# A gate table built from bfloat16 one-hots, with the gate split into three bfloat16 parts

## The chip, the cores and the metric

The kernel runs on one core of one Trainium2 chip. The metric is the device time of one execution in microseconds (us). A core has four compute engines with queues of their own, which run in order and wait for each other through semaphores: TensorE (PE in the profile, with its weight loads as PEld), VectorE (DVE), ScalarE (ACT) and GpSimd (POOL). SyncE (SP) issues most of the DMAs. [...]

## The reference, cut to what matters

One layer over 1024 frames of width 1024: two token mixers side by side (RWKV-7 and S5), then a mixture of 16384 single-neuron experts of which each of 8 heads picks 16 per frame, then a norm. The change lies in the expert part, between the choice of experts and their use.

```python
def _rms_norm(x, gain): ...                      # x * rsqrt(mean(x*x) + 1e-6) * gain
...
h = x                                             # (1, 1024, 1024)
p = _rms_norm(h, norm_mix) @ w_in                 # RWKV columns | S5 columns | two gates
y_a = _rwkv7_time_mix(p_rwkv, ...)                # recurrence over frames, 8 heads x 64
y_b = _s5_ssm_glu(p_s5, ...)
h = h + (g_a * y_a + g_b * y_b) @ w_out
h = h + _peer_ffn(_rms_norm(h, norm_ffn), ...)
return _rms_norm(h, norm_final)

def _peer_ffn(xn, wq, subkeys, table_u, table_v): # per block of 128 frames xt
    q = (xt @ wq).reshape(PEER_BLOCK, PEER_HEADS, 2, PEER_HALF)
    s = jnp.einsum('thcd,hcnd->thcn', q, subkeys)
    sv, si = lax.top_k(s, PEER_TOPK)              # 16 of 128 keys, on both sides
    cand = sv[:, :, 0, :, None] + sv[:, :, 1, None, :]
    cv, ci = lax.top_k(cand.reshape(PEER_BLOCK, PEER_HEADS, 256), PEER_TOPK)
    i1 = jnp.take_along_axis(si[:, :, 0], ci // PEER_TOPK, axis=-1)
    i2 = jnp.take_along_axis(si[:, :, 1], ci % PEER_TOPK, axis=-1)
    e = i1 * PEER_KEYS + i2                       # one of 128*128 experts
    gate = jax.nn.softmax(cv, axis=-1)
    hid = jax.nn.gelu(jnp.einsum('td,thkd->thk', xt, table_u[e]))
    return jnp.einsum('thk,thkd->td', gate * hid, table_v[e])
```

## The kernel before

The frames lie in eight blocks of 128. For the blocks 1 to 5 (`DB`) the experts are computed densely: every one of the 16384 experts is applied to all 640 frames, and a table of gates, zero where an expert was not chosen, weighs the result. The blocks 0, 6 and 7 (`GB`) fetch the rows of the chosen experts by indirect DMA instead, row by row.

`gate_table` makes the table of one dense block. For frame t the 128 chosen pairs (first key, second key) lie on the 128 partitions; a matrix product of two one-hot matrices, one of them scaled by the gates, adds each gate into its place of a 128 x 128 grid of experts. Four frames (`TG`) go at a time; such a step is called a group below, and there are 32 groups in a block and 160 in all. In a group VectorE compares an iota with the second keys (`oaq`) and with the first keys (`ohq`), in bfloat16; ScalarE copies `oaq` into the float32 tile `oha` in another order of axes; GpSimd or VectorE multiplies `ohq` by the gates `gT` into the float32 tile `ohb`; TensorE multiplies, one float32 product per frame, into the PSUM tile `gm`; ScalarE copies `gm` into a part of `stg`. Every eight groups `stg` (2 MB) is stored to the DRAM tensor `gd`.

No order is written out by hand. The functions run as streams of a planner, the class `Weave`, which has a cost for each instruction, keeps a queue time for each engine, and emits whichever ready instruction could start first, by a bonus for its stream where several could. `nc.copy` leaves the choice of ScalarE or VectorE to it, `nc.either` that of VectorE or GpSimd. The streams that matter here are `table` (the gate tables, bonus 2.0), `top` (the choice of experts, bonus 1.2), `front`, `pre` and `state` (the RWKV recurrence, 16 items, bonus 1.5 to 3.0) and `dense`.

`dense_stream` waits in the planner for the end of the RWKV streams. It then loads the frames `dx` (10 loads of 0.5 MB) and, chunk by chunk, the experts' first vectors `ur`; it splits each into `uh` (ScalarE) and `ul` (the rest, `ur - uh`), and computes the scores `S` of a chunk of 128 experts in 48 products. Scores of the first four chunks may run before the tables are done; `weigh` then multiplies the scores by the gates `G`, read back from `gd`, and the products into `acc` follow:

```python
            for _ in range(GV):
                next(X["ds"])

            wv.wait(lambda: {"tables", "top"} <= flags)
```

There are 128 chunks. The last instructions of an RWKV item are a group norm: the tile `ob`, its mean and variance (`m`, `rtrg`), the normed tile `yc`, eight small products `rs<-cst,yc`, and `y`, which SyncE stores to `ygd`.

Of the kernel before, what the change touches and what calls it, by code (L numbers as in the profile page):

```python
# [19 lines left out]
F32 = mybir.dt.float32  # L20
F32R = mybir.dt.float32r
BF = mybir.dt.bfloat16
# [3 lines left out]
OP = mybir.AluOpType  # L26
# [17 lines left out]
TG = 4  # L44
# [329 lines left out]
class Kern:  # L374
# [1147 lines left out]
    def gate_table(self, blk, e, g, pool):  # L1522


        nc, v = self.nc, self.nc.vector
        p = self.ps("gp", [128, 3, 128], 1, self.psg)
        for i, src in enumerate((e[:, :, 0], e[:, :, 1], g)):
            x = pool.tile([128, 128], F32, name=self.nm("slc"), tag="slc", bufs=1)
            nc.copy(x.rearrange("p (h k) -> p h k", h=8), src)
            nc.tensor.transpose(p[:, i], x, self.ident)  # L1530
        iT = pool.tile([128, 2, 128], BF, name=self.nm("iT"), tag="iT", bufs=2)
        gT = pool.tile([128, 128], F32, name=self.nm("gT"), tag="gT", bufs=2)
        nc.copy(iT, p[:, 0:2])
        nc.copy(gT, p[:, 2])
        for t32 in range(4):
            stg = pool.tile([128, 128, 32], F32, name=self.nm("stg"), tag="stg", bufs=2)
            for t16 in range(32 // TG):
                t0 = 32 * t32 + TG * t16
                shp = [128, 128, TG]
                bc = lambda x: x[:, None, t0:t0 + TG].to_broadcast(shp)  # L1540
                a, b = (pool.tile([128, TG, 128], F32, name=self.nm("oh" + x), tag="oh" + x, bufs=3) for x in "ab")
                turn = lambda x: x.rearrange("p t m -> p m t")
                bq = pool.tile(shp, BF, name=self.nm("ohq"), tag="ohq", bufs=2)
                aq = pool.tile(shp, BF, name=self.nm("oaq"), tag="oaq", bufs=2)
                v.tensor_tensor(aq, self.iotaM, bc(iT[:, 1]), op=OP.is_equal)
                nc.copy(turn(a), aq)
                v.tensor_tensor(bq, self.iotaM, bc(iT[:, 0]), op=OP.is_equal)
                nc.either("tensor_tensor", turn(b), bq, bc(gT), op=OP.mult)
                for t4 in range(TG // 4):
                    ps = self.ps("gm", [128, 4, 128], GMB, self.psg)  # L1550
                    for i in range(4):
                        t = 4 * t4 + i
                        nc.tensor.matmul(ps[:, i], a[:, t], b[:, t], start=True, stop=True)
                    o = TG * t16 + 4 * t4
                    nc.copy(stg[:, :, o:o + 4].rearrange("p i t -> p t i"), ps)
            nc.sync.dma_start(self.gd[4 * DB.index(blk) + t32], stg)
        self.tabled += 1

# [545 lines left out]
```

## Time and profile before

| | |
|---|---|
| median of 3 runs | 3673.98 us (3672.0 to 3679.5) |
| the profiled execution's own time | 3668.73 us |
| its span, first to last instruction | 3666.8 us |
| time outside the span | 1.9 us |
| granted clock of TensorE, mean | 0.944 |
| busy share PE / DVE / ACT / POOL | 90% / 77% / 38% / 33% |

The shares are means over stages with different limits. The gate tables are made between 1268 and 1635 us of the span, beside the end of the RWKV recurrence and of the choice of experts; the dense experts fill the time from there to the end. [...]

### The profile page before, as it was taken

The page shows a single profiled execution, that of the slowest core. Times are in us where ns is not written, and L with a number is a line of the kernel's source. Part 1 is how long each engine was busy: PE and PEld are TensorE (multiplying, and loading weights), DVE is VectorE, ACT ScalarE, POOL GpSimd, SP SyncE. Part 2 cuts the span into 40 slices and gives each one's busy share as a digit, 9 for nine tenths or more (in the row PEclk, how much of TensorE's full clock was granted, in tenths as well). Part 3 has the DMA queues.
Part 4 walks back from the last instruction along what each step waited for, and adds up shares of the span by engine and source line. Part 5 has one row for each costly group of instructions (what it writes and reads, how often), then busy time and mean ns, then how long its engine had stood idle before and what let it go on. Part 6 is the DMA issues. An engine that isn't in the chain of part 4 may idle for free.

```text
span 3666.8 us, 59750 instructions
## 1 busy us (share of the span) xinstructions
PE 3317.5 (90%) x22415; PEld 2841.2 (77%) x22415; DVE 2807.3 (77%) x6159; ACT 1398.3 (38%) x2906; POOL 1205.8 (33%) x1127
## 2 busy tenths in 40 slices
PE   7999999998888877778998889989999999999996
PEld 7777787767667766667887778878899998998985
DVE  7546412536989999956888968898888888888887
ACT  4322323323332398872333323323333333333333
POOL 3553323533443255432223222222222222223221
PEclk9899999998989898899999899989999999999998
DMA  5541223455567532268997789777898888988985
GB/s 207 199 165 64 87 91 114 136 174 176 194 238 258 181 126 116 117 203 296 330 329 275 266 311 346 281 278 284 296 326 304 320 317 317 323 305 293 323 298 219
DMA packets 359952, 869.10 MB, mean 237 GB/s; under 512 B 28960, under 2 KB 175520, under 8 KB 307952
## 3 DMA queue, kind: packets, MB, share of 16 engines
q1 hardware_dynamic: 303792, 461.01, 37.1%
q0 software_dynamic: 55296, 402.68, 29.3%
q8 instruction: 176, 2.88, 0.3%
q10 hardware_dynamic: 576, 1.61, 0.1%
q14 instruction: 112, 0.92, 0.1%
HBM read 759.16 MB, written 104.86 MB: 236 GB/s over the span
## 4 chain that ended last, share of the span: by engine, by line
PE 37%; DVE 25%; issue 16%; DMA 9%; ACT 6%; POOL 6%; SPq 1%; POOLq 0%; DVEq 0%; ACTq 0%
PE S L170 10%; PE acc L170 10%; PE mm L170 7%; POOL row L170 5%; PE tps L170 3%; DMA G<-gd 2%; DVE gacc L170 2%; DMA vr<-in_uv_dram 2%; ACT stg L170 2%; ACT oha L170 2%; PE rs L170 2%; PE gl L170 2%; DVE row L170 1%; PE pp L170 1%; PE rw L170 1%
## 5 line engine op out<-in xcount | busy, mean ns | idle before, releaser
L170 POOL DMA_INDIRECT row<-in_uv_dram,ei x384 | 524.8, 1367 | 1481.4 <-DVE gacc L170 1240.8
L170 PE MATMUL S<-dx,uh 128*128 128x320 f32 x4096 | 783.7, 313 | 14.1 <-ACT uh L170 7.5
L170 PEld LDWEIGHTS S<-dx,uh 128*128 128x128 f32 x4096 | 653.6, 190 | 32.6 <-ACT uh L170 9.9
L170 PE MATMUL acc<-vh,wh 128*128 128x512 f32 x1280 | 505.9, 403 | 55.8 <-DVE acc L170 49.0
L170 DVE SCALAR_TENSOR_TENSOR gacc<-row,hid,gacc 128x1024 f32<-128x1024 f32 x384 | 491.5, 1280 | 63.8 <-ACT hid L170 63.3
L170 PE MATMUL acc<-vl,wh 128*128 128x512 f32 x1280 | 513.2, 401 | 9.5 <-DVE vl L170 9.5
L170 PE MATMUL acc<-vh,wl 128*128 128x512 f32 x1280 | 509.7, 398 | 0.0
L170 PE MATMUL S<-dx,ul 128*128 128x320 f32 x2048 | 476.0, 313 | 19.3 <-DVE ul L170 15.4
L170 DVE CUSTOM_DVE_ANT_0 row<-row,gx 128x1024 f32<-128x1024 f32 x384 | 469.4, 1223 | 16.0 <-DMA row<-in_uv_dram,ei 15.8
L170 PEld LDWEIGHTS S<-dx,ul 128*128 128x128 f32 x2048 | 345.8, 190 | 25.6 <-DVE ul L170 19.1
L170 PEld LDWEIGHTS acc<-vh,wh 128*128 128x128 f32 x1280 | 245.1, 192 | 120.0 <-DVE acc L170 54.2
L170 ACT ACTIVATE hid<-hid 128x1 f32<-128x1 f32 x384 | 77.1, 201 | 576.6 <-DVE hid L170 576.0
L170 PEld LDWEIGHTS acc<-vl,wh 128*128 128x128 f32 x1280 | 246.7, 193 | 59.9 <-DVE vl L170 13.0
L170 PEld LDWEIGHTS acc<-vh,wl 128*128 128x128 f32 x1280 | 246.5, 193 | 54.9 <-issue 2.2
L170 ACT ACTIVATE vh<-vr 128x512 fp32r<-128x512 f32 x256 | 160.4, 627 | 315.4 <-PE acc L170 171.1
L170 PE MATMUL gm<-ohb,oha 128*128 128x128 f32 x1280 | 200.4, 308 | 57.3 <-ACT stg L170 38.2
L170 DVE TENSOR_TENSOR vl<-vr,vh 128x512 fp32r<-128x512 f32 x256 | 177.2, 693 | 90.3 <-ACT vh L170 88.3
L170 PEld LDWEIGHTS gm<-ohb,oha 128*128 128x128 f32 x1280 | 174.8, 213 | 75.7 <-issue 35.1
L170 DVE TENSOR_TENSOR acc<-acc,acc 128x512 f32<-128x512 f32 x320 | 213.6, 683 | 12.3 <-PE acc L170 11.7
L170 POOL TENSOR_TENSOR ohb<-ohq,gT 128x512 f32<-128x512 bf16 x126 | 151.5, 1204 | 155.0 <-DVE ohq L170 101.7
L170 PE MATMUL mm<-xnH,wh 128*128 128x512 f32 x480 | 196.3, 409 | 6.2 <-DVE pm L170 6.2
L170 PE MATMUL mm<-xnH,wl 128*128 128x512 f32 x480 | 194.7, 406 | 0.7 <-POOL wl L170 0.7
(443 smaller groups left out, 6280.9 us busy)
## 6 DMA issues: line engine op xcount, KB each, us to landing
ur<-in_ut_dram SPq DMA_DIRECT2D x128, 512.0 KB
vr<-in_uv_dram SPq DMA_DIRECT2D x256, 256.0 KB
wf<-wsd SPq DMA_DIRECT2D x120, 512.0 KB
gd<-stg SPq DMA_DIRECT2D x20, 2048.0 KB
G<-gd SPq DMA_DIRECT2D x31, 1280.0 KB
wsd<-sw SPq DMA_DIRECT2D x40, 512.0 KB
wr<-in_wc_dram SPq DMA_DIRECT2D x30, 512.0 KB
wr<-in_wg_dram SPq DMA_DIRECT2D x32, 256.0 KB
```

The lines of the kernel that those rows point to most:

```text
L170: op.alts = [(e, self.cost(e, n, outs, ins), lambda f=f, a=a, k=k: f(*a, **k)) for e, n, f, a, k in alts]
```

## The change

The two keys are compared in one VectorE instruction of 1024 elements, whose result `ohq` holds both one-hots in bfloat16. The gate is split, once per block, into three bfloat16 parts that add up to it (`gT`, with the rests `gr`); one VectorE instruction of 1536 elements multiplies the first one-hot by all three (`ohb`, also bfloat16). TensorE takes both as they lie, without the copies in another order of axes, and adds the three products of a frame in PSUM. The copy of `gm` into `stg` now reads PSUM in steps of 128 elements and writes runs of four, where before it read in order and wrote single elements 32 apart. The buffers of `ohq` and `ohb` are four each.

```diff
--- before.py
+++ after.py
@@ -1529,30 +1529,32 @@
             nc.copy(x.rearrange("p (h k) -> p h k", h=8), src)
             nc.tensor.transpose(p[:, i], x, self.ident)
         iT = pool.tile([128, 2, 128], BF, name=self.nm("iT"), tag="iT", bufs=2)
-        gT = pool.tile([128, 128], F32, name=self.nm("gT"), tag="gT", bufs=2)
+        gT = pool.tile([128, 3, 128], BF, name=self.nm("gT"), tag="gT", bufs=2)
         nc.copy(iT, p[:, 0:2])
-        nc.copy(gT, p[:, 2])
+        r = p[:, 2]
+        for k in range(3):
+            nc.copy(gT[:, k], r)
+            if k < 2:
+                r2 = pool.tile([128, 128], F32, name=self.nm("gr"), tag=f"gr{k}", bufs=1)
+                v.tensor_tensor(r2, r, gT[:, k], op=OP.subtract)
+                r = r2
         for t32 in range(4):
             stg = pool.tile([128, 128, 32], F32, name=self.nm("stg"), tag="stg", bufs=2)
             for t16 in range(32 // TG):
                 t0 = 32 * t32 + TG * t16
-                shp = [128, 128, TG]
-                bc = lambda x: x[:, None, t0:t0 + TG].to_broadcast(shp)
-                a, b = (pool.tile([128, TG, 128], F32, name=self.nm("oh" + x), tag="oh" + x, bufs=3) for x in "ab")
-                turn = lambda x: x.rearrange("p t m -> p m t")
-                bq = pool.tile(shp, BF, name=self.nm("ohq"), tag="ohq", bufs=2)
-                aq = pool.tile(shp, BF, name=self.nm("oaq"), tag="oaq", bufs=2)
-                v.tensor_tensor(aq, self.iotaM, bc(iT[:, 1]), op=OP.is_equal)
-                nc.copy(turn(a), aq)
-                v.tensor_tensor(bq, self.iotaM, bc(iT[:, 0]), op=OP.is_equal)
-                nc.either("tensor_tensor", turn(b), bq, bc(gT), op=OP.mult)
+                bc = lambda x: x[:, :, None, t0:t0 + TG].to_broadcast([128, x.shape[1], 128, TG])
+                oh = pool.tile([128, 2, 128, TG], BF, name=self.nm("ohq"), tag="ohq", bufs=4)
+                gb = pool.tile([128, 3, 128, TG], BF, name=self.nm("ohb"), tag="ohb", bufs=4)
+                v.tensor_tensor(oh, self.iotaM[:, None].to_broadcast([128, 2, 128, TG]), bc(iT), op=OP.is_equal)
+                v.tensor_tensor(gb, oh[:, 0:1].to_broadcast([128, 3, 128, TG]), bc(gT), op=OP.mult)
                 for t4 in range(TG // 4):
                     ps = self.ps("gm", [128, 4, 128], GMB, self.psg)
                     for i in range(4):
                         t = 4 * t4 + i
-                        nc.tensor.matmul(ps[:, i], a[:, t], b[:, t], start=True, stop=True)
+                        for k in range(3):
+                            nc.tensor.matmul(ps[:, i], oh[:, 1, :, t], gb[:, k, :, t], start=k == 0, stop=k == 2)
                     o = TG * t16 + 4 * t4
-                    nc.copy(stg[:, :, o:o + 4].rearrange("p i t -> p t i"), ps)
+                    nc.copy(stg[:, :, o:o + 4], ps.rearrange("p t i -> p i t"))
             nc.sync.dma_start(self.gd[4 * DB.index(blk) + t32], stg)
         self.tabled += 1
 
```

The planner makes a new order from this. The rows below are those of the program's order, before and after.

**VectorE, where the first table begins** (`ti`, `tv`, `t` belong to the choice of experts, `cs`, `cc`, `k`, `f`, `X`, `ob`, `yc` to RWKV). Before:

```order
L170 TENSOR_TENSOR oaq_13718<-iotaM,iT_13712 128x512
L170 TENSOR_TENSOR ohq_13717<-iotaM,iT_13712 128x512
L170 TENSOR_TENSOR oaq_13723<-iotaM,iT_13712 128x512
L170 TENSOR_TENSOR ohq_13722<-iotaM,iT_13712 128x512
L170 SCALAR_TENSOR_TENSOR cs_13766<-sreset,sa_13023 128x256
L170 TENSOR_TENSOR oaq_13798<-iotaM,iT_13712 128x512
L170 TENSOR_TENSOR cc_13767<-cs_13766 128x4x64
L170 TENSOR_TENSOR ohq_13795<-iotaM,iT_13712 128x512
L170 TENSOR_SCALAR cc_13767<-cs_13766 128x4
L170 SCALAR_TENSOR_TENSOR k_13771<-sa_13023,cols 128x256
```

And now:

```order
L170 TENSOR_TENSOR gr_13714<-gp_13674,gT_13713 128x128
L170 TENSOR_TENSOR ohq_13717<-iotaM,iT_13712 128x1024
L170 TENSOR_TENSOR ohq_13720<-iotaM,iT_13712 128x1024
L170 TENSOR_TENSOR gr_13715<-gr_13714,gT_13713 128x128
L170 TENSOR_TENSOR ohq_13723<-iotaM,iT_13712 128x1024
L170 SCALAR_TENSOR_TENSOR cs_13764<-sreset,sa_13023 128x256
L170 TENSOR_TENSOR ohb_13718<-ohq_13717,gT_13713 128x1536
L170 TENSOR_TENSOR ohb_13721<-ohq_13720,gT_13713 128x1536
L170 TENSOR_TENSOR ohb_13724<-ohq_13723,gT_13713 128x1536
L170 TENSOR_TENSOR ohq_13842<-iotaM,iT_13712 128x1024
L170 TENSOR_TENSOR cc_13765<-cs_13764 128x4x64
L170 TENSOR_TENSOR ohb_13843<-ohq_13842,gT_13713 128x1536
```

Before, two gate rows alternate with one to three rows of other streams all through the stage. Now 57 gate rows follow this piece with one row between them, and so it goes on: the tables of blocks 1 to 3 stand nearly without other work on VectorE, then some 230 rows of RWKV and of the choice of experts without a gate row, then the tables of blocks 4 and 5.

**VectorE, the end of the last RWKV item.** Before, the normed tile `yc` stands 81 gate rows ahead of the last one:

```order
L170 TENSOR_TENSOR rtrg_16491<-rtrg_16491 128x4 x2
L170 SCALAR_TENSOR_TENSOR rtrg_16491<-rtrg_16491 128x4
L170 TENSOR_TENSOR oaq_16819<-iotaM,iT_16276 128x512
L170 TENSOR_TENSOR ohq_16818<-iotaM,iT_16276 128x512
L170 TENSOR_TENSOR yc_16490<-ob_16246,rtrg_16491 128x256
L170 COPY slc_16833<-e_15958 128x128
L170 TENSOR_TENSOR oaq_16861<-iotaM,iT_16855 128x512
```

Now it stands behind the last gate row of all, `ohb_17917`:

```order
L170 TENSOR_REDUCE m_17448<-ob_17248 128x4
L170 TENSOR_TENSOR ohb_17917<-ohq_17916,gT_17307 128x1536
L170 TENSOR_SCALAR m_17448<-m_17448 128x4
L170 TENSOR_TENSOR ob_17248<-ob_17248,m_17448 128x256
L170 TENSOR_REDUCE m_17448<-yc_17449 128x4
L170 TENSOR_SCALAR m_17448<-m_17448 128x4
...
L170 TENSOR_TENSOR yc_17449<-ob_17248,rtrg_17450 128x256
L170 TENSOR_TENSOR vl_18146<-vr_18121,vh_18145 128x512
```

The dots stand for the eleven short operations that compute `rtrg`. On TensorE the eight products `rs<-cst,yc` of this item, and behind them the first score product, stand directly behind the last `gm` product; before, 29 rows of `S` stood among the `gm` rows.

**SyncE, the store of the last RWKV tile and the loads for the dense experts.** Before, the loads stand ahead of the last four stores of the table:

```order
L170 DMA gd<-stg_16696 128x4096
L170 DMA ygd_81<-y_16708 128x2x128
L170 DMA dx_16905<-xtT_84 128x8x128
...
L170 DMA ur_16907<-in_ut_dram 128x1024
L170 DMA gd<-stg_16857 128x4096
L170 DMA gd<-stg_16998 128x4096
L170 DMA ur_17158<-in_ut_dram 128x1024
L170 DMA gd<-stg_17111 128x4096
L170 DMA gd<-stg_17252 128x4096
```

Now they stand behind the last one:

```order
L170 DMA gd<-stg_17643 128x4096
L170 DMA gd<-stg_17789 128x4096
L170 DMA ygd_81<-y_17554 128x2x128
L170 DMA dx_18005<-xtT_84 128x8x128
...
L170 DMA ur_18007<-in_ut_dram 128x1024
L170 DMA ur_18023<-in_ut_dram 128x1024
L170 DMA ur_18058<-in_ut_dram 128x1024
L170 DMA vr_18121<-in_uv_dram 128x512
```

All ten `dx` loads and the four `ur` loads moved behind the twentieth store of the table and behind `ygd<-y`. From the first score on, GpSimd's order is the same as before, and that of the other engines nearly so.

## Rows read from the trace of the kernel before

**Rows 1.** Stretches: us; busy us (count) of PE PEld DVE ACT POOL; clock, DMA, GB/s.

```profile
1200.00:1267.00 67.00, 54.95 (x491) 48.52 (x489) 64.56 (x322) 17.52 (x41) 17.45 (x16) 0.82 0.66 220
1267.00:1560.00 293.00, 223.99 (x2143) 190.82 (x2143) 280.89 (x705) 263.32 (x353) 162.43 (x132) 0.90 0.28 112
1560.00:1635.00 75.00, 51.67 (x330) 45.27 (x329) 46.40 (x82) 64.60 (x76) 25.29 (x20) 0.89 0.62 205
2500.00:3500.00 1000.00, 987.71 (x5530) 897.30 (x5530) 865.26 (x1159) 351.14 (x828) 273.51 (x202) 1.00 0.87 312
```

**Rows 2.** Costliest groups, 1267 to 1640 us: what, count, busy us, mean ns, idle.

```profile
L170 PE MATMUL gm<-ohb,oha 128*128 128x128 f32 x1280 | 200.4, 308 | 57.3 <-ACT stg L170 38.2 <-DVE ohb L170 10.0 <-POOL ohb L170 6.5
L170 ACT ACTIVATE stg<-gm 128x512 f32<-128x512 f32 x160 | 180.4, 1142 | 16.1 <-PE gm L170 16.0
L170 ACT ACTIVATE oha<-oaq 128x512 f32<-128x512 bf16 x158 | 178.7, 1153 | 9.9 <-DVE oaq L170 9.6
L170 POOL TENSOR_TENSOR ohb<-ohq,gT 128x512 f32<-128x512 bf16 x126 | 151.5, 1204 | 155.0 <-DVE ohq L170 101.7 <-ACT sa L170 12.5 <-PE gm L170 8.0
L170 DVE TENSOR_TENSOR oaq<-iotaM,iT 128x512 bf16<-128x512 bf16 x160 | 100.9, 631 | 23.0 <-ACT oha L170 18.6 <-ACT iT L170 4.1
L170 DVE TENSOR_TENSOR ohq<-iotaM,iT 128x512 bf16<-128x512 bf16 x160 | 83.3, 521 | 1.0 <-POOL ohb L170 1.0
```

**Rows 3.** Timeline of ScalarE, 1589 to 1591 us: start, duration, what.

```profile
1589.10 1.17 ACT L170 ACTIVATE stg<-gm 128x512 f32<-128x512 f32 x1
1590.00 1.18 ACT L170 ACTIVATE oha<-oaq 128x512 f32<-128x512 bf16 x1
```

**Rows 4.** Timeline of VectorE at four places, with idle time in brackets.

```profile
1216.01 0.69 DVE L170 TENSOR_TENSOR oh<-rb,io 128x1024 bf16<-128x1024 bf16 x1
1216.61 0.15 DVE L170 TENSOR_SCALAR mst<-mst 128x1 f32<-128x1 f32 x1
...
1430.35 0.41 DVE L170 TENSOR_TENSOR oaq<-iotaM,iT 128x512 bf16<-128x512 bf16 x1
1430.69 0.41 DVE L170 TENSOR_TENSOR ohq<-iotaM,iT 128x512 bf16<-128x512 bf16 x1
...
1563.55 0.43 DVE L170 TENSOR_TENSOR oaq<-iotaM,iT 128x512 bf16<-128x512 bf16 x1 [3.64 <-ACT iT L170]
```

**Rows 5.** Timeline of TensorE: a `gm` group, the first and last scores, the first `acc`.

```profile
1440.93 1.16 PE L170 MATMUL gm<-ohb,oha 128*128 128x128 f32 x8
...
1601.12 0.85 PE L170 MATMUL S<-dx,uh 128*128 128x320 f32 x4 [0.61 <-ACT uh L170]
...
1653.26 0.57 PE L170 MATMUL S<-dx,uh 128*128 128x320 f32 x2 [0.38 <-ACT w L170]
...
1660.42 0.39 PE L170 MATMUL acc<-vh,wh 128*128 128x512 f32 x1
```

**Rows 6.** Timeline of the end of the last RWKV item, all engines.

```profile
1563.57 0.81 ACT L170 ACTIVATE y<-rs,cols 128x128 f32<-128x128 f32 x2
1564.45 0.78 POOL L170 TENSOR_TENSOR y<-y,bo 128x256 f32<-128x256 f32 x1 [4.62 <-ACT y L170]
1567.49 0.40 DVE L170 TENSOR_TENSOR y<-y,g 128x256 f32<-128x256 f32 x1
1567.97 0.37 SPq L170 DMA_DIRECT2D ygd<-y  x1
```

**Rows 7.** Timeline of SyncE's queue, and the last split of `ur`.

```profile
1568.45 16.29 SPq L170 DMA_DIRECT2D dx<-xtT  x10
1584.79 1.77 SPq L170 DMA_DIRECT2D ur<-in_ut_dram  x1
...
1646.14 0.33 SPq L170 DMA_DIRECT2D ur<-in_ut_dram  x1
...
1649.99 1.06 ACT L170 ACTIVATE uh<-ur 128x1024 fp32r<-128x1024 f32 x1 [5.79 <-DMA ur<-in_ut_dram]
...
1651.12 2.39 POOL L170 TENSOR_TENSOR ul<-ur,uh 128x1024 fp32r<-128x1024 f32 x1 [5.01 <-DMA G<-gd]
```

## The prediction

> **What bounds the kernel now.** I read the stretches first, because the shares over the whole span mix stages. From 2500 to 3500 us TensorE is busy 987.71 of 1000 us at the full clock [rows 1]: the dense experts are TensorE's, and whatever moves their start moves the end. The tables are made before that. From 1267 to 1560 us VectorE is busy 280.89 of 293 us and ScalarE 263.32; from 1560 to 1635 us VectorE falls to 46.40 of 75 and ScalarE stays at 64.60 [rows 1]. So the stage has two limits, VectorE while the choice of experts and RWKV still run beside the table, and ScalarE behind that.
>
> The groups of the stage say what fills them: on ScalarE the copies `oha` (178.7 us) and `stg` (180.4 us), on VectorE `oaq` and `ohq` with 160 instructions each, on GpSimd 126 `ohb` [rows 2]. The timeline gives the pace: a `stg` starts 0.90 us ahead of the `oha` behind it [rows 3], so a group of four frames costs ScalarE 1.80 us where it is the limit. On VectorE an `oaq` of 512 elements starts 0.34 us ahead of the next instruction when nothing disturbs it [rows 4], but the means are 631 and 521 ns [rows 2]: that is the stretch under GpSimd's work.
>
> What follows the stage matters as much. Scores need `dx` and `ur`, and before the change these are issued from 1568.45 us on, right behind `ygd<-y` at 1567.97 [rows 6, 7], 65 us ahead of the end of the stage. The first score runs at 1601.12 us, beside the tables, and the first `acc` at 1660.42 [rows 5]. That moment is what I forecast.
>
> **The change on VectorE.** 512 elements take 0.34 us and 1024 elements, of the same type and kind, 0.60 [rows 4], so another 512 cost 0.26 and 1536 cost 0.86. A group takes 0.60 + 0.86 = 1.46 us and 160 groups 234 us. The ten `gr` of 128 elements at some 0.3 add 3 us. The other work on VectorE: 705 + 82 instructions in the stage [rows 1], less 356 for the gates (160, 160, 34 `ohb`, 2 copies), leave 431; by the new order some 20 of them go to GpSimd, so 410. A like mix without gates cost 64.56 us for 322 instructions between 1200 and 1267 us [rows 1], 0.20 each: 82 us. About 3 us of it lie behind the last gate row. Without waits VectorE's last gate row would end at 1267 + 4 (the wait for the first `iT`, 4.1 us [rows 2]) + 234 + 3 + 79 = 1587 us.
>
> Waits come on top. In the new order the tables of blocks 1 to 3 lie together, then some 230 rows without a gate row, then blocks 4 and 5. At each of the last two blocks VectorE waits for the chain to `iT`, 3.64 us the last time [rows 4]: 7 us. In the middle piece (46 us of work) nothing fills the gaps of the recurrence and of the one-hot sums that GpSimd multiplies. The bounds are 2 us, by the 96% that VectorE was busy from 1200 to 1267 us, and 25, if it idled a third of the time; I take 12, nearer the first, since that stretch had this kind of work too. The last gate row then ends at 1587 + 7 + 12 = 1606 us.
>
> **The change on the other engines, at nothing.** ScalarE loses `oha` and keeps `stg`. Reading PSUM in steps is not in the trace. Below, 512 elements cost half of the 1.06 us of a plain copy of 1024 [rows 7]; above, I allow twice the present 0.90 us [rows 3]. I take 0.9, as the writes get easier and the reads harder: it hides behind VectorE's 1.46. At 1.8 it would not, and cost (1.8 - 1.46) x 160 = 54 us.
>
> [...]
>
> TensorE does 12 products of 128 columns per group instead of 8 (a float32 product is two in the trace: 1280 for 640 frames [rows 2]). Now 8 cost 1.16 us [rows 5], 0.145 each. [...] The bounds are 0.72 (128/320 of a score product) and 12 x 0.145 = 1.74 us. I take 0.83, as a bfloat16 product needs one pass like the score: hidden. [...] At 1.74 it costs 0.28 x 160 = 45 us. GpSimd's 151.5 us [rows 2] vanish; it was no limit, and what it gives back is counted in the undisturbed prices. The two extra copies and the rests `gr` per block lie ahead of the need, but for the waits above.
>
> **The work that the new order moves out.** The last RWKV item's `yc` stands behind the last gate row. Behind it come three long operations and some thirteen short ones, at 0.4 and 0.15 us [rows 4, 6], with one trip to ScalarE: about 5 us. Then `rs`, `y` on ScalarE (0.81), on GpSimd (0.78) and on VectorE (0.40) [rows 6], with the hops 3.5 us. So `ygd<-y` is issued 8 us behind the last gate row, and everything behind it in SyncE's queue waits: ten `dx` in 16.29 us, then `ur` [rows 7]. From the issue of a `ur` to its copy `uh` 3.85 us pass (1646.14 to 1649.99 [rows 7]). With a store of 2 MB just ahead, the first score starts about 8 + 17 + 4 + 2 = 31 us behind the last gate row. There is one buffer for `ur`: a load (3.85), `uh` (1.06) and `ul` (2.39) [rows 7] make 7.3 us a chunk, as much as its 48 products (7.16 [rows 5]). Four chunks and the wait for the first `ul` make 33 us. The first `acc` comes 64 us behind the last gate row. Nothing else can fill this on TensorE.
>
> **The sum.** First `acc` at 1606 + 64 = 1670 us, against 1660.4: 10 us later. The dense order is nearly the same from there on and TensorE-bound, so all of it reaches the end: 3668.7 of the profiled execution become 3679. That execution lies 5.3 us below the median of the runs, so I forecast 3674 + 10 = 3684 us. A measurement can tell about 0.2%, 7.3 us, from no change.
>
> **Rivals.**
> *The lost overlap is paid back, no change.* If the waits come to 10 instead of 19 us, or the tail to 55, the two nearly cancel: 3670 to 3681. VectorE's 96% speaks for it; that the middle piece has no filler speaks against it.
> *VectorE's other work gets cheap, faster.* Those 410 instructions may cost 0.15 instead of 0.20 us with less of GpSimd beside them, as `oaq` at 0.34 against a mean of 631 ns suggests [rows 2, 4]. That is 20 us less: the last gate row at 1586, the end at 3664. It decides from 17 us on. Against it: from 1200 to 1267 us, whence the 0.20, GpSimd was busy 17.45 of 67 us only [rows 1].
> *A new limit in the table.* `stg` or TensorE takes over from VectorE at 1.74 to 1.8 us a group, and the stage keeps about its present pace, with the work behind it still moved out: 45 to 54 us on top, 3729 to 3738. For `stg` it needs over 1.46 us, for a product 0.122.
> *The change does not do what it says* would be an `ohb` at half the rate of the comparisons: 0.52 us per further 512 elements instead of 0.26 [rows 4] are 0.78 us a group, 125 us. The comparisons read `iT` with the same broadcast, so I count it with the third rival, which it would overshoot.
>
> **How the numbers follow.** Forecast case (8 to 30 us later) 0.43, with its own range 3681 to 3704; paid back 0.28; faster 0.19; a new limit 0.10. So faster 0.19, same 0.28, slower 0.53. The likeliest case is at 3684. The range must reach to the fast rival and over the waits' bound of 25 us (3697) with a longer tail: 3661 to 3716 leaves out the best fast cases (0.07) and the new limit (0.10).
>
> **What would show it.** In the changed profile: `ohq` and `ohb` start 1.46 us apart per group, with GpSimd idle; ScalarE's `stg` is below that; the last `ohb` ends near 1606 us; `dx` is issued 8 us behind it; TensorE has a hole of some 25 us ahead of the first score; the first `acc` is near 1670 us, and 2000 us remain as before. I am wrong if a `stg` or a group of products paces the table, if the last `ohb` ends before 1590 or after 1625 us, or if the dense part itself changes length.

## The result, and the profile after

The changed kernel takes 3689.55 us (median of 20 runs, 3681.48 to 3704.47), the kernel before 3671.93 us beside it (20 runs, 3659.2 to 3680.65): a ratio of 1.0054, 95% interval 1.0043 to 1.0065. It is slower by 0.5%, 17.6 us, where 10 were forecast. The profiled execution has a span of 3687.3 us, 20.5 more than before.

The same stretches as in [rows 1], in the profile of the changed kernel:

```profile
core 0: us, PE busy (x) PEld busy (x) DVE busy (x) ACT busy (x) POOL busy (x), PEclk, DMA share, GB/s
1267.00:1560.00 293.00, 243.10 (x2460) 216.38 (x2459) 284.29 (x644) 106.18 (x223) 47.53 (x41) 0.84 0.26 107
1560.00:1635.00 75.00, 63.79 (x607) 58.74 (x605) 60.56 (x102) 27.98 (x55) 1.85 (x3) 0.88 0.40 164
2500.00:3500.00 1000.00, 985.32 (x5471) 894.65 (x5472) 861.88 (x1160) 346.96 (x817) 270.90 (x200) 0.99 0.88 309
```

ScalarE has fallen from 263 to 106 of 293 us, as meant. VectorE is as full as before, and TensorE is busy 243 us. The groups of the stage, 1267 to 1640 us, to be read beside [rows 2]:

```profile
L170 PE MATMUL gm<-ohb,ohq 128*128 128x128 bf16 x1920 | 235.1, 297 | 17.8 <-DVE ohb L170 17.8
L170 DVE TENSOR_TENSOR ohb<-ohq,gT 128x1536 bf16<-128x1536 bf16 x160 | 148.3, 965 | 0.0
L170 DVE TENSOR_TENSOR ohq<-iotaM,iT 128x1024 bf16<-128x1024 bf16 x160 | 106.6, 697 | 10.5 <-PE gm L170 6.3 <-ACT iT L170 4.0
L170 ACT ACTIVATE stg<-gm 128x512 f32<-128x512 f32 x160 | 95.8, 599 | 152.9 <-PE gm L170 152.9
```

A `stg` takes 0.60 us, where its mean before was above 1.1 [rows 2]: the steps are now in the read and not in the write, and it is ScalarE that waits, 152.9 us, for TensorE. The products `gm` fill TensorE for 235.1 us. The last gate rows on VectorE, with the end of the last RWKV item behind them:

```profile
1620.17 1.29 DVE L170 TENSOR_TENSOR ohq<-iotaM,iT 128x1024 bf16<-128x1024 bf16 x2
1621.38 1.82 DVE L170 TENSOR_TENSOR ohb<-ohq,gT 128x1536 bf16<-128x1536 bf16 x2
1623.11 0.68 DVE L170 TENSOR_TENSOR ohq<-iotaM,iT 128x1024 bf16<-128x1024 bf16 x1
...
1624.05 0.95 DVE L170 TENSOR_TENSOR ohb<-ohq,gT 128x1536 bf16<-128x1536 bf16 x1
...
1629.43 0.42 DVE L170 TENSOR_TENSOR yc<-ob,rtrg 128x256 f32<-128x256 f32 x1
```

Two groups start 2.94 us apart (1620.17 to 1623.11), 1.47 each. The last `ohb` ends at 1625.0 us. Before, it was one of GpSimd's and ended at 1627.9, three microseconds later:

```profile
1626.76 1.16 POOL L170 TENSOR_TENSOR ohb<-ohq,gT 128x512 f32<-128x512 bf16 x1 [2.46 <-DVE ohq L170]
```

What follows it in the changed kernel, on SyncE and on TensorE:

```profile
1633.56 0.37 SPq L170 DMA_DIRECT2D ygd<-y  x1
1634.04 14.93 SPq L170 DMA_DIRECT2D dx<-xtT  x10
1649.01 17.60 SPq L170 DMA_DIRECT2D ur<-in_ut_dram  x3
```

```profile
1617.70 9.27 PE L170 MATMUL gm<-ohb,ohq 128*128 128x128 bf16 x77
1629.91 1.12 PE L170 MATMUL rs<-cst,yc 64*64 64x64 f32 x16 [2.94 <-DVE yc L170]
1657.00 1.43 PE L170 MATMUL S<-dx,uh 128*128 128x320 f32 x4 [25.97 <-ACT uh L170]
...
1691.79 0.39 PE L170 MATMUL acc<-vh,wh 128*128 128x512 f32 x1
```

77 products start within 8.98 us, 76 intervals of 0.118 us, so a group of twelve costs TensorE 1.42 us (the expectations below have it as 0.117 and 1.41). Then TensorE has its hole of 25.97 us, and the first `acc` is at 1691.79 us against 1660.42 [rows 5]: 31.4 us late. At the end 20.5 are left.

### The profile page after: what moved, and what is told of

It is laid out like the page before. It is cut to its first block, busy times and chain, and to the rows that moved or that the text cites. A ratio compares the mean times of both kernels' runs of the same rounds, so it can differ in the third digit from the quotient of the medians.

```text
span 3687.3 us, 60437 instructions
## 1 busy us (share of the span) xinstructions
PE 3359.8 (91%) x23055; PEld 2891.3 (78%) x23055; DVE 2827.0 (77%) x6110; ACT 1210.2 (33%) x2761; POOL 1068.4 (29%) x1021
## 4 chain that ended last, share of the span: by engine, by line
PE 54%; DVE 24%; DMA 12%; issue 4%; ACT 3%; POOL 1%; SPq 1%; DVEq 0%; POOLq 0%; ACTq 0%
PE S L170 17%; PE acc L170 15%; PE mm L170 7%; PE gm L170 5%; DMA G<-gd 4%; PE tps L170 3%; DVE gacc L170 2%; DMA vr<-in_uv_dram 2%; PE rs L170 2%; PE gl L170 2%; DVE row L170 2%; DVE oh L170 1%; PE pp L170 1%; PE rw L170 1%; SPq L170 1%
## 5 line engine op out<-in xcount | busy, mean ns | idle before, releaser
L170 DVE SCALAR_TENSOR_TENSOR gacc<-row,hid,gacc 128x1024 f32<-128x1024 f32 x384 | 491.5, 1280 | 61.5 <-ACT hid L170 61.2
L170 PE MATMUL gm<-ohb,ohq 128*128 128x128 bf16 x1920 | 235.1, 297 | 17.8 <-DVE ohb L170 17.8
L170 PEld LDWEIGHTS <-ohq 128*128 128x128 bf16 x1920 | 217.2, 118 | 31.2 <-DVE ohb L170 13.4
L170 PE MATMUL mm<-xnL,wh 128*128 128x512 f32 x480 | 194.1, 404 | 0.0
```

The source lines that it names most:

```text
L170: op.alts = [(e, self.cost(e, n, outs, ins), lambda f=f, a=a, k=k: f(*a, **k)) for e, n, f, a, k in alts]
```

## The experiments

All have the changed kernel as their base, but for the one that says otherwise. Most are read by the same marks: the end of the last `ohb`, the first score and the first `acc`. These marks come from one profiled execution of each kernel, the times from several runs.

**Two orders with the scores beside the tables.** The dense experts' buffers need room that the gate tables have taken; three buffers free it, and stand alone as a control (`small`):

```diff
-        gT = pool.tile([128, 3, 128], BF, name=self.nm("gT"), tag="gT", bufs=2)
+        gT = pool.tile([128, 3, 128], BF, name=self.nm("gT"), tag="gT", bufs=1)
-                oh = ... tag="ohq", bufs=4)
-                gb = ... tag="ohb", bufs=4)
+                oh = ... tag="ohq", bufs=3)
+                gb = ... tag="ohb", bufs=3)
```

> The changed kernel with three buffers of ohq and of ohb instead of four each and one gT instead of two, nothing else; the order of every engine stays the same. It is the control for the two kernels with another order, which need the room. My theory (VectorE paces the tables at 1.47 us a group, TensorE follows at 1.41 us, one group behind): no more than 3 us from the changed kernel, 3685 to 3693 us, waits of VectorE for gm below 12 us. Rival (TensorE's 1.41 us so near to VectorE's 1.47 that a buffer less makes VectorE wait for it): waits for gm over 25 us, the last ohb at 1645 us or later, over 3702 us.

Measured: 3710.48 us, ratio 1.0081 (1.0051 to 1.0111), with one of the four runs at 3691.86 us and the others at 3710 to 3711; the last `ohb` at 1647.2, the first `acc` at 1713.7 us. The theory fell, the rival was right: VectorE's waits for TensorE in this stage are 63 instead of 9, and 22.7 us instead of 6.3, a little under the rival's 25.

```profile
DVE ohq L170 <- PE gm L170: 22.7, 63, 1.8
```

With `BO` of the table stream lowered as well (`rwkv_sooner`), and with RWKV first (`rwkv_first`):

```diff
-            BO = [1.0, 1.0, 1.0, 2.8, 1.2, 2.0, -3.0, -2.0, 0.0] + ...
+            BO = [1.0, 1.0, 1.0, 2.8, 1.2, 1.0, -3.0, -2.0, 0.0] + ...
```

```diff
-        X["need"], NDL = 2, 12
+        X["need"], NDL = 2, 16
```

> As the control, with the planner's bonus of the table stream at 1.0 instead of 2.0: the last RWKV item goes ahead of the last 100 of the 160 gate groups, and dx, ur and the first scores stand beside the tables. My theory (the loss is the work that the change moved behind the tables, since VectorE's sum is the same in either order): the last ohb at 1625 us give or take 10, the first score ahead of it, no hole of 26 us on TensorE, the first acc some 27 us behind the end of the tables as before the change, so near 1655 instead of 1692 us; of these 37 us two thirds reach the end, as 31.4 us at the first acc became 20.5 at the end: 3658 to 3672 us, ratio to before 0.996 to 1.000. Rival (the scores beside the tables cost the tables as much, through TensorE, which has only 0.06 us a group to spare): the last ohb at 1650 us or later, 3684 to 3695 us.

> As the control, with the last four RWKV items at the bonus of the others (NDL 16 instead of 12): all of RWKV ahead of nearly all gate groups. My theory: the scores overlap fully, but the recurrence loses the gate rows that filled its gaps on VectorE, so the last ohb moves 10 to 30 us later, to 1635 to 1655 us, and the first acc to 1655 to 1675; 3660 to 3685 us. Rival (as for the other order, TensorE's spare time decides): the last ohb at 1660 us or later, over 3690 us.

Measured: 3712.09 us, ratio 1.0100 (1.0081 to 1.0120), and 3727.29 us, 1.0137 (1.0115 to 1.0158). In `rwkv_sooner` the first score is at 1507.3 us and the first `acc`, at 1699.5, only 20 us behind the last `ohb`, as expected of the overlap; but the last `ohb` moved to 1679.1 us, 32 later than in the control, and the four chunks take 4 x 7.2 = 29 us of TensorE. VectorE's waits:

```profile
DVE ohq L170 <- PE gm L170: 43.2, 46, 7.6
```

So of the 46 us by which the first `acc` moved closer to the last `ohb` (20.4 instead of 66.5 us), 32 were paid at the last `ohb`. The other 14 stand at the first `acc` of this one execution, and the times show nothing of them: the two intervals of `rwkv_sooner` and `small` overlap. In `rwkv_first` the last `ohb` is at 1695.7, with 67 waits of VectorE for `gm`. In both my theory, that the late end comes from the order alone, fell, and the last `ohb` is where the rivals had it; the time of `rwkv_sooner` lies above its rival's 3684 to 3695 us too, as that of the control does.

**The same order in the kernel before.**

> The kernel before, with the same change of order alone (NDL 16). My theory: before the change ScalarE sets the pace of the tables where they stand alone (1.80 us a group), so that taking RWKV out from beside them lengthens the stage: 3690 to 3730 us. Rival (the order alone is worth what it brings the changed kernel): 3640 to 3665 us.

Measured: 3722.81 us, ratio 1.0125 (1.0099 to 1.0151), as the theory had it. The tables, from 1348 to 1678 us, take 2.06 us a group with the scores between them, and not 1.80; ScalarE is busy 310 of these 330 us, VectorE 296.

**Which engine paces the tables: two by two.** VectorE or TensorE does two of the three gate parts, or both do; the order of the instructions is kept.

```diff
-                v.tensor_tensor(gb, oh[:, 0:1].to_broadcast([128, 3, 128, TG]), bc(gT), op=OP.mult)
+                v.tensor_tensor(gb[:, :2], oh[:, 0:1].to_broadcast([128, 2, 128, TG]), bc(gT[:, :2]), op=OP.mult)
```

```diff
-                            nc.tensor.matmul(..., start=k == 0, stop=k == 2)
+                            mm = nc.tensor.real.matmul if k < 2 else lambda *a, **kw: None
+                            nc.tensor.w.issue(("PE", "matmul", mm, (...), dict(start=k == 0, stop=k == 1)))
```

> The changed kernel, VectorE multiplying two of the three gate parts (1024 elements instead of 1536), TensorE still with 12 products a group (the third takes the first part again, so the gates are wrong); the planner counts the old cost, so the order stays. VectorE would need 1.20 us a group instead of 1.47, TensorE 1.41 as now. If VectorE alone paces the tables (my theory at the prediction): the last ohb 40 us earlier, near 1585 us, and the end 25 to 35 us earlier, 3655 to 3665 us. If TensorE stands right behind it (what the run with three buffers suggests): the last ohb 5 to 15 us earlier, VectorE's waits for gm up from 6 us to over 30, 3677 to 3688 us.

> The changed kernel, TensorE adding two of the three parts (8 products a group, the last 8 bits of the gates are left out), VectorE still making all three; the order stays. TensorE would need 0.94 us a group. If VectorE alone paces the tables: the last ohb no more than 6 us earlier (the waits for gm go), 3682 to 3690 us. If the two share the limit: 8 to 20 us earlier, 3672 to 3682 us.

> Both: two parts on VectorE and on TensorE, the third left out, the order as in the changed kernel. VectorE 1.20 us a group, TensorE 0.94. Every theory expects the last ohb about 42 us earlier, near 1583 us; with the work behind it as long as now and a third given back in the dense part, 3650 to 3662 us. Were the work behind it tied to something else than the last ohb (gathers, the tables' stores), the end would move by less than 15 us.

| | last `ohb`, us | first `acc`, us | median, us | ratio to before |
|---|---|---|---|---|
| changed kernel | 1625.0 | 1691.8 | 3689.55 | 1.0054 (1.0043 to 1.0065) |
| VectorE two | 1615.4 | 1683.2 | 3683.80 | 1.0031 (1.0014 to 1.0049) |
| TensorE two | 1617.4 | 1683.7 | 3681.52 | 1.0018 (0.9999 to 1.0036) |
| both two | 1580.0 | 1644.9 | 3648.34 | 0.9941 (0.9917 to 0.9964) |

Either alone brings 8 to 10 us at the last `ohb`, both together 45. That is what two engines of nearly the same pace look like. One thing more differs between these runs: from 1277 to 1330 us, early in the tables, the granted clock (1.00 is the full one) is 0.91 in the changed kernel and 0.92 with VectorE alone at two parts, but 0.55 with TensorE alone at two and 0.65 with both, so TensorE's other work may have taken back part of the 8 us. With two parts on VectorE it waits for TensorE instead:

```profile
DVE ohq L170 <- PE gm L170: 29.9, 64, 1.3
```

**What makes a product cost 0.118 us.** The products read neighbouring elements, in both operands (`packed_products`) or in `ohq` alone (`packed_weights`):

```diff
-  oh[:, 1, :, t], gb[:, k, :, t]
+  oh[:, 1].rearrange("p m t -> p (m t)")[:, 128 * t:128 * t + 128], gb[:, k].rearrange(...)[:, 128 * t:128 * t + 128]
```

> The changed kernel with products that read 128 neighbouring elements of ohq and ohb instead of every fourth (the numbers that are multiplied are then wrong, the shapes and the order stay). If the step of four elements makes a product 0.117 us instead of the 0.069 that I had worked out: a product near 0.07, a group of twelve near 0.83 us, and the time as with two parts on TensorE. If it is the load of 128 columns of weights for each product: still 0.112 to 0.117 us, as the products of the kernel before took 0.112, and 3685 to 3693 us.

> As with the packed products, for ohq alone (the stationary operand): ohb is read at every fourth element again (the products are wrong, shapes and order stay). If it is the load of the weights that the step slows: 0.056 us a product. If it is the moving operand: 0.117 us. Between the two, if both count.

Two groups of twelve at the end of the tables, with packed products, and 46 products with packed weights alone:

```profile
1605.61 1.71 PE L170 MATMUL gm<-ohb,ohq 128*128 128x128 bf16 x24 [1.23 <-DVE ohb L170]
```

```profile
1602.74 5.51 PE L170 MATMUL gm<-ohb,ohq 128*128 128x128 bf16 x46
```

Packed, a group costs less than 0.86 us and TensorE waits 1.23 of every 2.94 us; the median of the start intervals is 0.056 us, below the 0.07 expected. With packed weights it stays at 0.116. So the step of the moving operand, `ohb`, 8 bytes between elements, is enough for the price, and packing `ohq` beside it takes off no more than 0.002 us. Whether a stepped `ohq` would cost something beside a packed `ohb` was not run. `packed_products` took 3675.97 us, ratio 1.0012 (0.9997 to 1.0027), its last `ohb` at 1611.2; `packed_weights`, a single run of 3678.76 us, has its last `ohb` at 1623.2 like the changed kernel.

**A layout that TensorE reads well and VectorE still writes well.** Four frames lie as two pairs, so that a product reads every second element; the tables are complete.

```diff
-        gT = pool.tile([128, 3, 128], BF, ...)
+        gT = pool.tile([128, 64, 3, 2], BF, ...)
-                gb = pool.tile([128, 3, 128, TG], BF, ...)
+                gb = pool.tile([128, 2, 3, 128, 2], BF, ...)
-  oh[:, 1, :, t], gb[:, k, :, t]
+  oh[:, i // 2, 1, :, i % 2], gb[:, i // 2, k, :, i % 2]
```

> The changed kernel with ohq and ohb laid out in pairs of frames, so that a product reads every second element (4 bytes apart) instead of every fourth (8 bytes); all three parts, the right gates, the order as in the changed kernel. If the price of a product follows the step (0.056 us at a step of one, 0.117 at four): 0.056 to 0.09 us, a group below 1.1 us, and as with the packed products the last ohb near 1611 us and 3672 to 3682 us, provided that VectorE still takes 0.60 and 0.87 us for a run of two. If any step makes TensorE slow: 0.117 us and 3685 to 3693 us. If VectorE loses its rate with runs of two elements: 2.5 us or more a group and over 3800 us.

The timeline of TensorE and VectorE near the end of the tables, and the stretch of the tables:

```profile
1603.09 1.73 PE L170 MATMUL gm<-ohb,ohq 128*128 128x128 bf16 x24 [1.21 <-DVE ohb L170]
```

```profile
1600.88 1.28 DVE L170 TENSOR_TENSOR ohq<-iotaM,iT 128x1024 bf16<-128x1024 bf16 x2
1602.09 1.82 DVE L170 TENSOR_TENSOR ohb<-ohq,gT 128x1536 bf16<-128x1536 bf16 x2
```

```profile
1267.00:1614.00 347.00, 219.91 (x3083) 179.00 (x3082) 342.47 (x753) 133.10 (x283) 82.89 (x42) 0.86 0.29 119
```

A product costs 0.057 us and VectorE's price is unchanged; VectorE is busy 342.47 of 347 us, so hardly anything else limits the stage. The last `ohb` is at 1614.5 and the first `acc` at 1680.9 us, 10.9 sooner. But the median is 3689.74 us, ratio 1.0044 (1.0028 to 1.0061): the expected 3672 to 3682 us were missed, and the run is not told apart from the changed kernel, although `packed_products`, with a like gain at the marks, is 14 us faster than the changed kernel. In this profile the dense part took 2006.3 us, in that of the changed kernel 1995.5.

**Pairs and the other order.** The pairs with the planner's bonus of 1.0 for the tables and three buffers of `ohq` and `ohb`.

> The pairs of frames (products at 0.057 us) together with the order in which the last RWKV item and the first scores go ahead of the last gate groups, and three buffers of ohq and ohb. My theory now (VectorE and TensorE shared the limit of the stage; what kept the other order from paying was TensorE's 1.41 us a group): TensorE has 0.75 us a group to spare, so the 30 us of scores fit beside the tables; the last ohb at 1612 to 1632 us instead of 1679, the first acc some 20 us behind it, at 1630 to 1655 us; the end, with 1990 to 2006 us from there, at 3635 to 3660 us, faster than both kernels. Rival (the order itself costs: the recurrence moved forward leaves VectorE without filler, or the scores' copies take its time): the last ohb at 1645 us or later, 3670 us or more. Second rival (the dense part takes it back, as it took back the 11 us of the pairs): the first acc early as said, but 3670 us or more at the end.

Measured: 3667.57 us, ratio 0.9981 (0.9963 to 0.9999); the last `ohb` at 1640.0 and the first `acc` at 1658.8 us. It is 22 us faster than the changed kernel and a little faster than the one before. All three ranges of the theory were missed, by 8 us at the last `ohb`, 4 at the first `acc` and 8 at the end. The first score costs more than its products, as it stands in TensorE's queue ahead of gate products and waits there for its load; VectorE waits behind it:

```profile
1488.81 1.14 PE L170 MATMUL gm<-ohb,ohq 128*128 128x128 bf16 x14
1496.47 1.44 PE L170 MATMUL S<-dx,uh 128*128 128x320 f32 x4 [6.52 <-ACT uh L170]
```

```profile
1503.28 0.69 DVE L170 TENSOR_TENSOR ohq<-iotaM,iT 128x1024 bf16<-128x1024 bf16 x1 [9.46 <-PE gm L170]
```

So the theory holds in its sign, and both rivals take their part of it: the overlap pays with the cheaper products, the order costs VectorE (the last `ohb` is 25 us later than in `pairs`, part of it perhaps by the buffer less), and of the 33 us at the first `acc` 24 reach the end of the span.

**The same with two gate parts.**

> Pairs of frames and the order with the scores beside the tables, as in the last run, with two gate parts on VectorE and TensorE (the third, the last 8 bits of the gates, is left out) and four buffers again. If VectorE alone is left as the limit of the stage: 160 times 0.27 us less, the last ohb 35 to 45 us ahead of the 1640 us of the last run, at 1595 to 1605, the first acc 20 us behind it, the end at 3620 to 3640 us. Rival (the scores and their loads now hold the stage): the last ohb at 1615 us or later, 3645 us or more, no better than two parts alone (3648).

Measured: 3632.53 us, ratio 0.9899 (0.9876 to 0.9922); the last `ohb` at 1593.1, the first `acc` at 1610.9 us. The last `ohb` is 47 us sooner than with three parts, where 43 were worked out for VectorE, and 35 us of that reach the end: the rival fell, and the gain is about VectorE's. What the fourth buffer adds to it is not separated, and VectorE is busy 297 of the 326 us from 1267 us on, so it is not the only limit left.

## Why the prediction was right, and where it was not

**VectorE's pace for a gate group** was forecast at 1.46 us and is 1.47. **ScalarE** was put at 0.9 us a group and takes 0.60, hidden, so the third rival failed on ScalarE. Its 1.8 us there was my estimate, twice the 0.90 of before. Reading PSUM in steps of 128 elements and writing runs of four this copy takes 0.60 us, where reading in order and writing single elements took 1.1. That the stepped read would be harder was my estimate too. What the stepped read costs by itself is not shown, as both sides of the copy changed.

**TensorE at 0.83 us a group, hidden, is the step that failed.** The 0.83, which is 0.069 a product, was my estimate between two bounds, and no run shows it. A product of this kernel costs 0.118 us, a group 1.42, inside my upper bound of 1.74. The estimate left out the step of 8 bytes at which the products read `ohb`: with a packed operand a product costs 0.056 us (`packed_products`), 0.67 a group, below even my lower bound of 0.72. At 1.42 TensorE still lies below VectorE's 1.47, so by my sum it cost nothing; in truth the two have 0.05 us between them, and RWKV's products on TensorE come on top. The two-by-two runs show it: take it from TensorE alone and the last `ohb` comes 8 us sooner, or 14 with packed products.

**The last `ohb`** was forecast at 1606 us and ended at 1625.0. In the changed kernel's trace, from 1267 to 1625 us:

```profile
1267.00:1625.00 358.00, 303.80 (x3034) 272.54 (x3033) 341.46 (x729) 131.85 (x273) 47.93 (x42) 0.85 0.28 116
```

VectorE is idle 358.0 - 341.5 = 16.5 us, against the 23 that I had put there (4 for the first `iT`, 7 at block boundaries, 12 in the middle piece). The gates would take 160 x 1.47 = 235 us and take 241, counted from each row's start to the next; the few that lie beside GpSimd's work are longer (8 `ohq` with a mean of 0.97 us, the others 0.68). The ten `gr` take 2. The other 399 instructions take the rest, 98 us, 0.25 each, against 79: this is the term that was mis-sized, by 19 us. The 0.20 came from a stretch full of short choices of experts; here long RWKV operations and one-hot sums are among them (32 `oh` rows of 0.60 each). The waits were smaller than assumed by 6.5 us, and would be some 4.5 without TensorE's price (`pairs`), so that the 12 us for the middle piece came out by luck: they stood for a wait that was mostly TensorE's. The rival that VectorE's other work gets cheap was wrong in its sign.

**The tail** was close in all its parts. `ygd<-y` is issued 8.6 us behind the last `ohb` (8 forecast), ten `dx` take 14.93 us (16.29), the first score comes 32 us behind the last `ohb` (31), TensorE's hole is 25.97 us ("some 25"), and the first `acc` comes 66.8 us behind (64). One part I did not list lies in it: behind its hole TensorE's granted clock is 0.53 from 1657 to 1666 us and 1.00 behind that, and the first chunk of scores takes 12.3 us where the three behind it take 7.2 to 7.7. A score product starts every 0.267 us where the clock is 0.50 and every 0.147 us where it is 1.00 (medians of the changed kernel).

```profile
1657.00:1666.00 9.00, 8.00 (x30) 7.60 (x31) 0.00 (x0) 2.34 (x2) 4.48 (x2) 0.53 0.17 58
1666.00:1690.00 24.00, 22.86 (x152) 22.07 (x151) 6.43 (x6) 6.65 (x12) 6.47 (x5) 1.00 0.79 257
```

**"All of it reaches the end" did not come out either.** The first `acc` was 21.8 us later than the 1670 forecast, and 31.4 later than before; 20.5 are left at the end of the span, 17.6 in the medians. In the profiles the 11 us are given back between 1890 and 2510 us, where TensorE was not full. Before and after:

```profile
1890.00:2510.00 620.00, 551.34 (x2925) 482.34 (x2924) 529.93 (x1047) 187.82 (x456) 152.51 (x109) 0.93 0.82 294
```

```profile
1890.00:2510.00 620.00, 561.90 (x3025) 492.07 (x3024) 545.34 (x1079) 197.40 (x478) 158.04 (x115) 0.95 0.85 301
```

TensorE is busy 10.6 us more in the changed kernel. So the forecast of 3684 us is close partly because two errors, +22 at the first `acc` and -11 behind it, have opposite signs. Whether the change gives these 11 us back by a cause of its own stays open: from the first `acc` to the end the profiled executions took 2006.4 us before, 1995.5 after, 2006.3 with the pairs and 1987.2 with `packed_weights`, one execution each, and runs of the changed kernel alone spread over 23 us. The 32 chunks of that stretch, from the start of the 17th copy `uh` to that of the 49th, took 593 us before and 578 after, and 572 to 595 in the other twelve profiles, so that the difference is within the spread of single executions.

**The sign** follows from the moved work, as forecast: the tables end at nearly the same time (1625.0 against 1627.9 us), and what ran beside them comes behind, so that the first `acc` is 66.8 us behind the tables instead of 32.5. The order before was less mixed than I had told it: its last 79 gate rows on VectorE, from 1558 us on, already stood nearly without other rows between them, and of the first four `ur` loads only two, at 1584.79 and 1604.16 us, were issued ahead of the table's last store. But the order is not the cause alone. With TensorE as dear as it is, putting the scores back beside the tables brings nothing in the times (`rwkv_sooner` against its control); with the pairs it brings 22 us, though with a buffer less than in `pairs`. At the first `acc`, in single executions, the two differ less, 14 and 22 us, so how much of the order's worth TensorE's price takes is not settled.

**Of my signs of being wrong** two came out in part, and one stands at its mark: TensorE shares the pace of the table with VectorE, the dense part was 11 us shorter in the profile, and the last `ohb` ended at 1625.0 us. The time was inside the range; the mechanism was right in VectorE's pace and in the tail, and wrong in TensorE and in VectorE's other work.

## What to carry to other kernels

When work is taken from the engine that limits a stage, list what every other engine then needs for one unit, from rows of the same operand layout, and not of the same instruction alone: here two engines at 1.42 and 1.47 us acted as one limit, and a repair of either showed little until both were repaired. Work that is put back beside the stage is worth its time only as far as the engines there have room, so that an order should be judged after the prices, not before. A moved first instruction of a later stage also holds whatever stands behind it in its queue, here gate products behind a score that waited 6.52 us for its load.

## What the runs showed of the hardware

The records of TensorE's granted clock, in the kernel before and in the changed one, hold two shares only, 1.00 and 0.50. A bfloat16 gate product is one record in the changed kernel's trace (1920 for 1920) and a score product one (6144 for 6144), where a float32 gate product was two (1280 for 640).

At the full clock, 1.00, a bfloat16 product of 128 columns took 0.056 us with a packed moving operand, 0.057 with its elements 4 bytes apart and 0.118 with 8 bytes; with 8 bytes in the moving operand, packing the stationary one changed next to nothing (0.116). At 0.50 the products with 8 bytes started every 0.118 us in the changed kernel, as at 1.00: the lower clock cost the stepped products nothing. The float32 records of the kernel before, whose operands are packed, started every 0.112 us at 1.00 and every 0.213 at 0.50. With fewer products, as in the run with two parts on TensorE alone, the granted clock from 1600 to 1620 us was 0.50, and the products with the step of 8 bytes cost the same, 0.118 us:

```profile
1600.00:1620.00 20.00, 13.46 (x104) 11.27 (x104) 19.27 (x35) 8.19 (x14) 0.00 (x0) 0.50 0.33 136
...
1600.09 2.06 PE L170 MATMUL gm<-ohb,ohq 128*128 128x128 bf16 x16 [0.88 <-DVE ohb L170]
```

VectorE took 0.60 and 0.87 us for 1024 and 1536 bfloat16 elements whether the gates were read in runs of four or of two elements. Beside GpSimd's work it was slower: in the kernel before, the 105 `oaq` that overlap with it took 0.74 us in the mean and the other 55 took 0.42. A ScalarE copy of 512 elements out of PSUM took 0.60 us when it read steps of 128 elements and wrote runs of four.
